# A hybrid attention trunk on one core: matmul order of all heads written out, and three smaller edits

## The chip, the cores and the metric

The kernel runs on one core of a Trainium2 chip. The core has a matmul engine (PE, TensorE), three engines for elementwise work (VectorE or DVE, ScalarE or ACT, GpSimd or POOL), a queue that issues transfers (SP) and 16 DMA engines. The engines run side by side, each through its own list of instructions in order, and wait for each other through semaphores. The metric is the device time of one execution in microseconds (us). The kernel before takes 1009.78 us, the median of three runs (1008.76 to 1011.21).

## What is computed

Four layers act on x, 512 tokens by 1024 features in float32. Layer 0 and 3 use latent attention (MLA), layer 1 a sliding window of 128 with sinks (SWA), layer 2 forgetting attention (FoX). Each has 16 heads, a SiLU gate on the heads' outputs, an output projection, and a residual with a layer norm. Cut to what matters:

```python
def _mla_branch(x, w_in, q_norm, w_q_up, kv_norm, w_kv_up, w_out):
    h = x @ w_in                                   # cq 384, ckv 256, k_rope 32, gate 1024
    q = (_rmsnorm(cq, q_norm) @ w_q_up).reshape(B, S, 16, 64 + 32)
    kv = (_rmsnorm(ckv, kv_norm) @ w_kv_up).reshape(B, S, 16, 64 + 64)
    q_rope = _apply_rope(q[..., 64:], cos, sin)
    k_rope = _apply_rope(k_rope, cos, sin)         # one rotated key of 32, shared by all heads
    o = _dense_causal(q_full, k_full, v, 96 ** -0.5)
    return (o * silu(gate)) @ w_out

def _apply_rope(x, cos, sin):
    x1, x2 = split(x, 2)
    return concat([x1 * cos - x2 * sin, x2 * cos + x1 * sin])
# SWA: 16 query heads on 4 key heads, 128-query blocks against 256 keys, ALiBi; the sink joins the maximum:
    m = maximum(max(s), sink); p = exp(s - m) / (sum(exp(s - m)) + exp(sink - m))
# FoX: dense causal softmax with a cumulative log forget gate added to the scores
# every layer: x = layernorm(alpha * x + branch(x))
```

## The kernel before, in words

**Tiles.** Every float32 operand of a matmul is split into a rounded part and a remainder (fp32r), and a product is made of three matmuls (two for scores whose halves are stacked). Weights come from memory in units of up to 128 x 1024 by SP; ACT makes the rounded part (L291) and GpSimd, or VectorE for the output projection, the remainder (L295). `W` asks for a unit and has the following three prepared too (L302). A projection writes one bank of PSUM (three banks rotate, tag pp) and is then taken out by ACT and VectorE.

**A head.** Four score blocks s0 to s3 (one for each 128 queries, L450 or L903); after each a masked minimum on VectorE (L843, L904, L1023 and L1025; the scores are negated, so it stands for the maximum). `softmax_tail` (L415) is emitted after s3: in SWA the sink minimum (L419), exponentials on ACT with sums (L421), in SWA the sink's term (L424, L425), the reciprocal (L427), and the scaling of the first three blocks on GpSimd (L432) and of the last on ACT (L430). Then the probabilities are transposed on the matmul engine: three groups t0, t1, t2 (keys 0, 1, and 2 with 3) in MLA and FoX, two groups in SWA. t0 needs all four blocks in MLA and FoX, the first three in SWA. Each group is taken from its bank by ACT (L466) and VectorE (L467, remainder at L310). The product with V (pv, `attn_pv`) uses one bank; its result is added up by ACT and VectorE (L504, L505), and after each second head multiplied with the gate on GpSimd (L512) and split into oT for the output projection.

**Order.** `run_heads` (L614) emits, for h from 0 to 13, the scores of head h + 1, then the transposes and pv of head h, and between them steps of one stream: the projections of the later heads in the order of STREAM, then the first part of the output projection (`out_part`). FILLS holds how many steps go into each head. This emission order sets priorities; a planner that replays the program with its own costs settles the order on every engine, matmul too, and ANCHOR holds each stream step behind a named step of an earlier head (`held`). Only the last two heads (`tail`) and the start of MLA have the matmul order as written. FINISH is a written order for the end of a layer; its f entries run further steps of the output projection.

**MLA's start.** `t_block` makes cq, ckv and the shared key for each block of 128 tokens in two units of 352 columns: 672 columns of weights and, a second time, the 32 key columns with their halves swapped. `t_norm` scales, and rotates the key by four VectorE operations on 64 or 32 columns (L740 to L744), which also write its negative. `tr_kr` transposes the result (L774). V is projected in four units of 256 columns, each for four heads (`vproj`, `vp`).

Of the kernel before, what the change touches and what calls it, by code (L numbers as in the profile page):

```python
# [46 lines left out]
ANCHOR = (('s', 0), ('s0', 0), ('s', 1), ('o', 2))  # L47
TAIL = ((3, 4, 6, 6), (2, 10, 2, 5), (9, 0, 4, 9), (6, 3, 7, 2))
# [3 lines left out]
T_COLS = 352  # L52
# [3 lines left out]
def jobs(s):  # L56
# [11 lines left out]
FILLS = (  # L68
# [4 lines left out]
)  # L73


def layer_units(kind):
# [8 lines left out]
    for n, a in FIRST[kind] + STREAM[kind]:  # L85
        if kind == 0 and n in "KQR":
            p = 2 * a if n == "R" else a
            new = [("QK", p, 0, 640 if p % 2 else SUB)]
        elif kind == 0 and n == "V":
            new = [("V", a, 0, 512)]  # L90
        else:
            new = [("V", a, b, SUB) for b in range(2)] if n == "V" else [(n, a, 0, SUB)]
# [16 lines left out]
def pack_weights(inp):  # L109
# [8 lines left out]
    for (layer, n, a, b), off, c in units:  # L118
        kind, j = layer % 3, layer // 3
        if kind == 0:  # L120
            w_in, w_out = inp["mla_w_in"][j], inp["mla_w_out"][j]
            if n == "T":
                ro = QR + KR
                kr = w_in[:, ro:ro + 32]
                ks = np.concatenate([kr[:, 16:], kr[:, :16]], 1)
                w = np.concatenate([w_in[:, :ro], kr, ks], 1)[:, a * T_COLS:(a + 1) * T_COLS]
# [11 lines left out]
            elif n == "V":  # L138
                wv = inp["mla_w_kv_up"][j].reshape(KR, H, 128)[:, 4 * a:4 * a + 4, 64:].reshape(KR, 256)
# [25 lines left out]
def shape_consts():  # L165
# [7 lines left out]
    cc = np.concatenate([cos, cos, cos, -cos], 1)  # L173
    ss = np.concatenate([sin, sin, -sin, sin], 1)
    krt = np.stack([cc, ss], 1).reshape(NT, 128, 2, 64).transpose(1, 0, 2, 3).astype(np.float32)
# [12 lines left out]
class Net:  # L188
    def __init__(self, ctx, tc, t):
# [32 lines left out]
        self.cq_free = 0  # L222
        self.hold = len(units)
# [82 lines left out]
    def mm(self, out, l, r, start, stop):  # L306
        self.last = self.nc.tensor.matmul(out, l, r, start=start, stop=stop).ins  # L307
# [87 lines left out]
    def vproj(self, keys, nk, lhs, store, qd, tbs=range(NT), extra=None):  # L395
        per = -(-nk // len(keys))
        n = VF_COLS if extra else 256
        ps = None
        for tb in tbs:
            ws = [self.W(*k) for k in keys]  # L400
            if qd not in store:
                store[qd] = self.p_vo.tile([128, NT, 4, 128], F32R, tag="vo", name=self.nm("v"))
            if tb % 2 == 0 or extra or ps is None:
                ps = self.bank()
            c0 = 0 if extra else tb % 2 * 256
            out = ps[:, c0:c0 + n]
            yield from self.tokproj_steps(out, lambda k: (ws[k // per], (k % per) * n), n, lhs, tb, range(nk), True, True,
                                            8 if nk == 8 else 6)
            self.v_fin(store[qd], out[:, :256], tb)
# [203 lines left out]

    def run_heads(self, layer, st, make, pre=iter(()), npre=3):  # L614

        st["order"] = chain(chain.from_iterable(make[n](a) for n, a in STREAM[layer % 3]), self.out_part(layer, st))
        st["P"], st["PT"], st["oT"] = {}, {}, []
        marks = {}
        what, lag = ANCHOR[layer]

        def held(gen, h):

            after = marks.get((what, h - lag))
            with self.tc.issue_after(after) if after is not None else nullcontext():
                next(gen, None)

# [3 lines left out]
        marks["s", 0] = self.last  # L630
        self.run(pre)
        for h in range(H - 2):
            sn, tn = st["s_fn"](h + 1, st), st["t_fn"](h, st)
# [463 lines left out]
```

## Time and profile before

| | |
|---|---|
| median of three runs | 1009.78 us |
| the profiled execution's own time | 1010.33 us |
| its span, first to last instruction | 1008.5 us |
| mean granted matmul clock | 0.992 |
| PE busy | 981.8 us, 97%, 5512 matmuls |
| weight loads (PEld) busy | 857.3 us, 85% |
| DVE, ACT, POOL busy | 607.1, 620.8, 501.3 us |
| DMA | 117.31 MB |

The busy times are of one profiled execution. Busy time of PE is the union of matmuls that overlap in the pipeline; the time between starts of neighbouring matmuls tells how fast they go. A row of a group names line, engine, operation, tile written <- tiles read, shape and count, then busy us and mean ns of one, then the engine's idle time before them. In the timeline a row holds start, length, engine, line, operation, tiles, shape and count of neighbouring instructions put together. MLA's first pairs and heads lie at about 61 to 220 us, SWA's at 294 to 424, FoX's at 524 to 722, the second MLA's at 808 to 957.

### The profile page before, as it was taken

The numbers are of one execution on the slowest core, as the hardware profiler recorded it, in microseconds if no ns is written. First come the engines' busy times: TensorE is split into PE (matmuls) and PEld (weight loads), VectorE is DVE, ScalarE is ACT, GpSimd is POOL, SyncE is SP. The second block draws the span as 40 slices with busy tenths as digits, with TensorE's granted clock in tenths as the row PEclk, the third lists the DMA queues.
The fourth block names the chain that finished last, engine by engine and source line by source line (L and its number), as shares of the span: only waits on it lengthen the run. The fifth ranks groups of instructions, "written<-read, shape, count | busy, mean of one in ns | idle before, by whom it ended". The sixth has DMA issues, their size and how long they took to land.

```text
span 1008.5 us, 16186 instructions
## 1 busy us (share of the span) xinstructions
PE 981.8 (97%) x5512; PEld 857.3 (85%) x5512; DVE 607.1 (60%) x1533; ACT 620.8 (62%) x1354; POOL 501.3 (50%) x524
## 2 busy tenths in 40 slices
PE   8999999999999999999999999999999999999995
PEld 7988898888988888788988898888789888888784
DVE  2567666854636667729324655567457676668727
ACT  4378798854256777723446766566433588888722
POOL 4645665334145663423455757553252656664213
PEclk9999999999999999999999999999999999999998
DMA  6353333552542222334344334325234444324312
GB/s 222 125 140 105 92 103 95 150 172 97 188 126 84 80 68 102 111 92 158 96 141 131 105 85 145 106 78 192 88 104 136 121 130 125 97 84 134 97 64 84
DMA packets 37795, 117.31 MB, mean 116 GB/s; under 512 B 5440, under 2 KB 5440, under 8 KB 37456
## 3 DMA queue, kind: packets, MB, share of 16 engines
q1 hardware_dynamic: 37712, 116.27, 37.7%
q8 instruction: 44, 0.72, 0.3%
q14 instruction: 39, 0.32, 0.1%
HBM read 93.15 MB, written 8.42 MB: 101 GB/s over the span
## 4 chain that ended last, share of the span: by engine, by line
PE 48%; DVE 2%; issue 2%; ACT 1%; POOL 1%; DMA 0%; SPq 0%; DVEq 0%; POOLq 0%; ACTq 0%
PE pp L307 32%; PE ss L307 5%; PE oo L307 4%; PE po L307 4%; PE ptt L480 3%; DVE r L594 1%; POOL r L610 1%; PE pxt L357 1%; DMA q<-rq 0%; DVE r L546 0%; PE pc L764 0%; DVE w L295 0%; ACT wo L291 0%; DVE kt L310 0%; DVE wo L295 0%
## 5 line engine op out<-in xcount | busy, mean ns | idle before, releaser
L307 PE MATMUL pp<-xT,w 128*128 128x512 f32 (+1 forms) x1440 | 352.6, 387 | 0.1
L295 POOL TENSOR_TENSOR w<-wr,w 128x512 fp32r<-128x512 f32 (+1 forms) x202 | 242.5, 1226 | 197.0 <-ACT w L291 125.7
L307 PEld LDWEIGHTS pp<-xT,w 128*128 128x128 f32 x1440 | 256.2, 188 | 44.5 <-ACT xT L361 0.3
L432 POOL TENSOR_TENSOR P<-P,rs 128x256 f32<-128x256 f32 (+2 forms) x192 | 112.9, 616 | 134.5 <-DVE rs L427 130.8
L291 ACT CAST w<-wr 128x1024 fp32r<-128x1024 f32 (+5 forms) x121 | 116.6, 967 | 84.4 <-PE pp L307 44.1
L421 ACT ACTIVATE P<-P,m 128x256 f32<-128x256 f32 (+3 forms) x256 | 137.8, 539 | 47.6 <-DVE m L843 16.8
L310 DVE TENSOR_TENSOR PT<-ptt,PT 128x384 fp32r<-128x384 f32 (+1 forms) x176 | 103.7, 600 | 46.5 <-ACT PT L466 45.2
L307 PE MATMUL pp<-w,xT 128*128 128x256 f32 (+2 forms) x768 | 114.3, 302 | 3.1 <-ACT xT L361 2.5
L307 PEld LDWEIGHTS pp<-w,xT 128*128 128x128 f32 x768 | 107.4, 190 | 4.9 <-ACT xT L361 2.9
L466 ACT CAST PT<-ptt 128x384 fp32r<-128x384 f32 (+1 forms) x176 | 88.2, 515 | 35.3 <-PE ptt L480 24.8
L307 PE MATMUL oo<-PT,v 128*128 128x256 f32 (+3 forms) x512 | 106.6, 313 | 3.1 <-DVE o L505 2.9
L307 PEld LDWEIGHTS oo<-PT,v 128*128 128x128 f32 x512 | 83.4, 189 | 13.8 <-DVE o L505 3.4
L307 PE MATMUL ss<-kt,q 128*128 128x128 f32 (+3 forms) x384 | 81.5, 328 | 2.3 <-ACT kt L796 1.6
L307 PE MATMUL pp<-cT,w 128*128 128x512 f32 x312 | 81.6, 397 | 0.0
L480 PE MATMUL ptt<-ident,P 128*128 128x128 f32 x480 | 79.3, 277 | 1.3 <-POOL P L432 1.3
L307 PE MATMUL pp<-w,oT 128*128 128x512 f32 x288 | 76.4, 400 | 0.0
L843 DVE CUSTOM_DVE_ANT_0 P<-ss,mask 128x128 f32<-128x128 f32 (+3 forms) x128 | 60.9, 484 | 25.2 <-PE ss L307 20.7
L307 PE MATMUL po<-wo,oT 128*128 128x512 f32 x288 | 71.5, 396 | 0.0
L307 PEld LDWEIGHTS ss<-kt,q 128*128 128x128 f32 x384 | 60.6, 189 | 8.7 <-ACT kt L796 2.2
L480 PEld LDWEIGHTS ptt<-ident,P 128*128 128x128 f32 x480 | 57.7, 142 | 11.1 <-POOL P L432 1.8
L505 DVE TENSOR_TENSOR o<-oo,o 64x512 f32<-64x512 f32 x64 | 43.9, 686 | 38.0 <-ACT o L504 34.0
L307 PEld LDWEIGHTS pp<-cT,w 128*128 128x128 f32 x312 | 56.6, 188 | 10.3
(121 smaller groups left out, 1427.5 us busy)
## 6 DMA issues: line engine op xcount, KB each, us to landing
wr<-in_w SPq DMA_DIRECT2D x106, 512.0 KB, 3.6
q<-rq SPq DMA_DIRECT2D x64, 128.0 KB, 2.4
xd<-r SPq DMA_DIRECT2D x12, 512.0 KB, 2.8
r<-xd SPq DMA_DIRECT2D x12, 512.0 KB, 3.5
wr<-in_w SPq DMA_DIRECT2D x16, 352.0 KB, 3.5
kd<-kd SPq DMA_DIRECT2D x20, 256.0 KB, 3.0
tq<-in_cs SPq DMA_DIRECT2D x8, 512.0 KB, 3.8
cb<-cd SPq DMA_DIRECT2D x16, 256.0 KB, 3.7
```

Of the source, the lines that this page charges most:

```text
L291: nc.scalar.copy(w[0][:, :c], r[:, :c])
L295: eng.tensor_tensor(w[1][:, a:b], r[:, a:b], w[0][:, a:b].bitcast(F32), op=ALU.subtract)
L307: self.last = self.nc.tensor.matmul(out, l, r, start=start, stop=stop).ins
L310: (eng or self.nc.vector).tensor_tensor(out, src, hi.bitcast(F32), op=ALU.subtract)
L357: nc.tensor.transpose(v, xt[:, c:c + 128], self.ident[:])
L421: nc.scalar.activation(v, v, AF.Exp, bias=m[:, c:c + 1], scale=-1.0, accum_out=sums[:, c:c + 1])
L432: nc.gpsimd.tensor_tensor(v, v, rs[:, c:c + 1].to_broadcast([128, v.shape[1]]), op=ALU.mult)
L466: nc.scalar.copy(pt[:, 0, :n], ps[:, :n])
L480: nc.tensor.transpose(ps[:, c:c + 128], Ps[qb][:, kb * 128:(kb + 1) * 128], self.ident[:])
L505: nc.vector.tensor_tensor(o[a, :], o_ps[a, :], o[a, :], op=ALU.add)
L594: nc.vector.scalar_tensor_tensor(r[:, cols], in0=src[:, cols], scalar=s[:, k:k + 1], in1=st["gb"][2 * part + c][:], op0=op, op1=(ALU.mult, ...
L843: nc.vector.tensor_tensor_reduce(out=P[:, :n], in0=ps[:, :n], in1=self.mask[:, S - n:], scale=1.0, scalar=3e38, op0=ALU.add, op1=ALU.min, ...
```

## The change

- **Order of the heads.** `run_heads` puts all heads under a written matmul order. STREAM, FILLS, ANCHOR and `tail` give way to PAIRS: for each pair of heads, the projections that are made during it. The steps of a head stand as s0 s1 t0 s2 t1 s3 t2 pv (s of head h + 1, the others of head h; without t2 in SWA), and after each step so much of the pair's projections is emitted that their columns keep up with the share of steps done. EXTRA steps of the output projection join in the last pair; TAIL tells the steps of it after each step of the last two heads. The other engines are still ordered by the planner.
- **336-column units.** The swapped copy of the key columns is no longer projected; T_COLS is 336.
- **Key rotation on GpSimd.** Two products of 32 columns and four sums or differences of 16 in place of four VectorE operations.
- **512-wide V in MLA.** Two units of 512 columns, each for eight heads; the first is made ahead of the pairs and the second in the second pair.
- FINISH of layer 3 starts with f22 in place of f14.

```diff
-    'f14 k0 k1 k2 f99 r0 r1 s0 s1 ...
+    'f22 k0 k1 k2 f99 r0 r1 s0 s1 ...
...
-ANCHOR = (('s', 0), ('s0', 0), ('s', 1), ('o', 2))
-TAIL = ((3, 4, 6, 6), (2, 10, 2, 5), (9, 0, 4, 9), (6, 3, 7, 2))
+
+TAIL = (
+    (1, 1, 1, 1, 1, 1, 2, 3, 2, 2, 3),
+    (1, 1, 2, 1, 2, 2, 3, 3, 3),
+    (2, 1, 2, 1, 2, 1, 2, 3, 3, 2, 3),
+    (1, 1, 1, 1, 1, 1, 2, 3, 2, 2, 3),
+)
...
-T_COLS = 352
+T_COLS = 336
...
-STREAM = (
-    jobs("K1 Q1 R1 K2 Q2 V1 G2 K3 Q3 G3 R2 K4 Q4 V2 G4 K5 Q5 G5 R3 K6 Q6 V3 G6 K7 Q7 G7"),
-    jobs("G0 Q2 G1 Q3 G2 Q4 G3 Q5 G4 Q6 G5 Q7 G6 G7"),
-    jobs("Q2 K2 Q3 K3 G2 Q4 K4 V2 G3 Q5 K5 G4 Q6 K6 G5 V3 Q7 K7 G6 G7"),
+PAIRS = (
+    ("K1 Q1 R1 G2", "K2 Q2 V1", "K3 Q3 R2 G3", "K4 Q4 G4", "K5 Q5 R3 G5", "K6 Q6 G6", "K7 Q7 G7"),
+    ("G0 Q2", "G1 Q3", "G2 Q4", "G3 Q5", "G4 Q6", "G5 Q7", "G6 G7"),
+    ("V2 Q2 K2", "G2 Q3 K3", "G3 Q4 K4", "V3 Q5 K5", "G4 Q6 K6", "G5 Q7 K7", "G6 G7"),
 )
+STREAM = tuple(jobs(" ".join(k)) for k in PAIRS)
+
+EXTRA = (3, 0, 8, 3)
...
     def mm(self, out, l, r, start, stop):
-        self.last = self.nc.tensor.matmul(out, l, r, start=start, stop=stop).ins
+        self.nc.tensor.matmul(out, l, r, start=start, stop=stop)
+        self.cols += max(256, out.shape[-1])
...
+    def job_cols(self, kind, n, a):
+
+        if kind == 0 and n in "KQR":
+            return (6 if n == "K" else 9) * 512
+        return 96 * 256 if n == "V" and kind else 24 * 512
+
+    def slots(self, layer, st, h):
+
+        sn = st["s_fn"](h + 1, st) if h + 1 < H else []
+        tn = st["t_fn"](h, st)
+        out = sn[:2] + tn[:1] + sn[2:3] + tn[1:2] + sn[3:] + tn[2:]
+        return out + [lambda: self.attn_pv(h, st)]
+
     def run_heads(self, layer, st, make, pre=iter(()), npre=3):
 
-        st["order"] = chain(chain.from_iterable(make[n](a) for n, a in STREAM[layer % 3]), self.out_part(layer, st))
+        with self.tc.manual_schedule(engines={mybir.EngineType.PE}):
+            self.heads(layer, st, make, pre, npre)
+
+    def heads(self, layer, st, make, pre, npre):
+        kind = layer % 3
+        st["order"] = self.out_part(layer, st)
...
+        for p in range(NP - 1):
+            todo = jobs(PAIRS[kind][p])
+            total = sum(self.job_cols(kind, n, a) for n, a in todo)
+            gen = chain.from_iterable(make[n](a) for n, a in todo)
+            if p == NP - 2:
+                gen = chain(gen, islice(st["order"], EXTRA[layer]))
+                total += EXTRA[layer] * 3 * 512
+            done = i = 0
+            for h in (2 * p, 2 * p + 1):
+                steps = self.slots(layer, st, h)
+                for f in steps:
                     f()
+                    i += 1
+                    while done + 768 < total * i / (2 * len(steps)):
+                        c = self.cols
+                        if next(gen, self) is self:
+                            break
+                        done += self.cols - c
+            self.run(gen)
+        self.cq_done(layer)
+        steps = self.slots(layer, st, H - 2) + self.slots(layer, st, H - 1)
+        for f, n in zip_longest(steps, TAIL[layer], fillvalue=0):
+            f()
+            self.run(islice(st["order"], n))
         self.finish(layer, st)
...
-            a, b = x[:, 640:704], x[:, 704:768]
-            nc.vector.tensor_tensor(b, a, krt[:, tb, 1, :], op=ALU.mult)
-            nc.vector.tensor_tensor(a, a, krt[:, tb, 0, :], op=ALU.mult)
-            nc.vector.tensor_tensor(x[:, 768:800], x[:, 640:672], x[:, 736:768], op=ALU.add)
-            nc.vector.tensor_tensor(x[:, 800:832], x[:, 672:704], x[:, 704:736], op=ALU.add)
+            kr, c, d = x[:, 640:672], x[:, 672:704], x[:, 704:736]
+            nc.gpsimd.tensor_tensor(c, kr, krt[:, tb, 0, :], op=ALU.mult)
+            nc.gpsimd.tensor_tensor(d, kr, krt[:, tb, 1, :], op=ALU.mult)
+            c1, c2, d1, d2 = x[:, 672:688], x[:, 688:704], x[:, 704:720], x[:, 720:736]
+            for o, l, r, op in ((768, c1, d2, ALU.subtract), (784, c2, d1, ALU.add), (800, c2, d1, ALU.add), (816, d2, c1, ALU.subtract)):
+                nc.gpsimd.tensor_tensor(x[:, o:o + 16], l, r, op=op)
...
-        vp = lambda qd, tbs=range(NT): self.vproj([(layer, "V", qd, 0)], 2, vlhs, vs, qd, tbs)
+        vp = lambda a, tbs=range(NT): self.vproj([(layer, "V", a, 0)], 2, vlhs, vs, (2 * a, 2 * a + 1), tbs)
```

`vproj` now takes a list of groups of four heads: for MLA it makes 512 columns per block in a bank of its own, and hands each half to its group's `v_fin` (ACT and VectorE).

More of the change, by code (lines that the diff above doesn't have):

```diff
@@ L1 @@
 import math
-from contextlib import ExitStack, nullcontext
-from itertools import chain, islice
+from contextlib import ExitStack
+from itertools import chain, islice, zip_longest
 import numpy as np
@@ L89, in layer_units @@
         elif kind == 0 and n == "V":
-            new = [("V", a, 0, 512)]
+            new = [("V", a, 0, SUB)]
         else:
@@ L222, in __init__ @@
         self.cq_free = 0
+        self.cols = 0
         self.hold = len(units)
@@ L984, in fox @@
         vs, qt, kt = {}, {}, {}
-        vp = lambda qd, tbs=range(NT): self.vproj([(layer, "V", qd, 0), (layer, "V", qd, 1)], 8, self.xblk, vs, qd, tbs)
+        vp = lambda a, tbs=range(NT): self.vproj([(layer, "V", a, b) for b in range(2)], 8, self.xblk, vs, (a,), tbs)
         z = self.p_g.tile([128, NT, H], F32, tag="g", name=self.nm("z"))
@@ L992, in fox @@
         for tb in range(NT):
-            self.run(self.vproj([(layer, "V", 0, b) for b in range(3)], 8, self.xblk, vs, 0, [tb], f_logit))
+            self.run(self.vproj([(layer, "V", 0, b) for b in range(3)], 8, self.xblk, vs, (0,), [tb], f_logit))
             self.run(vp(1, [tb]))
```

72 lines of the change are left out of this document (18 added, 54 removed), and 6 rows, old and new, of tables (FILLS, FINISH).

## The prediction

> **What bounds the kernel now.** I read the page first, then the waits of the matmul engine, then the merged chain that ended last. The page's busy line, and its shares of the chain by engine and by line:
>
> ```profile
> PE 981.8 (97%) x5512; PEld 857.3 (85%) x5512; DVE 607.1 (60%) x1533; ACT 620.8 (62%) x1354; POOL 501.3 (50%) x524
> ...
> PE 48%; DVE 2%; issue 2%; ACT 1%; POOL 1%; DMA 0%; SPq 0%; DVEq 0%; POOLq 0%; ACTq 0%
> ```
>
> Matmul is on the chain far more than any other engine. The waits of that engine over the whole span (total us, times, longest):
>
> ```profile
> PE oo L307 <- DVE o L505: 2.9, 2, 1.6
> PE pp L307 <- ACT xT L361: 2.5, 1, 2.5
> PE pxt L357 <- DVE r L594: 2.4, 4, 1.0
> PE ss L307 <- DVE m L904: 1.6, 3, 0.7
> PE ss L307 <- ACT kt L796: 1.6, 2, 0.8
> ...
> PE ptt L480 <- POOL P L432: 1.3, 3, 0.6
> PE ss L307 <- DVE m L843: 0.8, 3, 0.4
> ```
>
> They are small: what a new order of the heads can win back is oo 2.9 + ss 1.6 + ptt 1.3 + ss 0.8 = 6.6 us; xT, pxt and kt belong to the stages between and to the first scores of a layer. That the engine is full when it does not wait shows in the merged chain (start, length, count):
>
> ```profile
> 538.58 0.76 PE ptt L480 x7
> ...
> 584.26 2.93 PE pp L307 x24
> ...
> 734.87 8.30 PE po L307 x36
> ```
>
> The first are transposes, at 0.76/7 = 0.109 us each, the second 256-column matmuls at 2.93/24 = 0.122 us, the third 512-column ones at 8.30/36 = 0.231 us. I use these spacings below, since the busy times of single matmuls overlap. The heads are therefore bound by matmul issue, and any wait that a rigid order adds there is added to the end.
>
> **Columns saved.** Groups by form:
>
> ```profile
> L307 PE MATMUL pp<-xT,w 128*128 128x512 f32 x1344 | 339.7, 394 | 0.0
> L307 PE MATMUL pp<-w,xT 128*128 128x352 f32 x288 | 50.6, 329 | 3.1 <-ACT xT L361 2.5 <-DVE xT L310 0.3 <-ACT w L291 0.3
> L307 PE MATMUL pp<-w,cT 128*128 128x256 f32 x192 | 28.7, 286 | 0.1
> ```
>
> From 352 to 512 columns a matmul gets (394 - 329)/160 = 0.41 ns per column longer, so 16 columns less are 6.5 ns. There are 2 layers x 4 blocks x 2 units x 24 = 384 of them: **-2.5 us**. V of MLA goes from 192 matmuls of 256 to 96 of 512: 192 x 0.122 - 96 x 0.231 = **-1.2 us**. Part of V moves out of the pairs' stream into the stage ahead of the heads; that is a shift on the same engine and costs nothing more. The weight casts and subtractions become fewer or shorter.
>
> The Trainium skill ("Trainium Kernel Development and Optimization", Performance Expectations, and "Perfetto Trace Analysis", Identifying the Most-Contended Engine) says that matmul busy time is a bad measure and that the busy share of weight loads is a good one. By that rule the 85% above would leave some 15% of the span free, both this saving and the waits below could vanish in it, and the sum would be zero; by the spacing of the chain the engine is full and they count in whole.
>
> **Rotation of the shared key.** Four VectorE operations per block become six on GpSimd, of 32 and 16 columns. The nearest rows:
>
> ```profile
> L743 DVE TENSOR_TENSOR cqk<-cqk 128x32 f32<-128x32 f32 x8 | 3.4, 427 | 0.0
> ...
> L295 POOL TENSOR_TENSOR w<-wr,w 128x32 fp32r<-128x32 f32 x1 | 0.3, 257 | 0.0
> ```
>
> Six at up to 0.26 us are 1.5 us a block on GpSimd. Its reader is the transpose pkr, late in this piece of the matmul timeline:
>
> ```profile
> 44.95 5.63 PE L307 MATMUL pp<-xT,w 128*128 128x512 f32 x24
> ...
> 61.31 0.60 PE L774 MATMUL pkr<-ident,cqk 128*64 128x128 f32 x4
> ```
>
> The last block is projected before 44.95 and read at 61.31: 16 us of gate, transposes and projections cover it. Queued behind it on GpSimd are weight remainders loaded three units ahead. I take zero; with the cover gone it would be 1.5 us in each of two layers, 3 us.
>
> **The order of the heads.** Now the three transposes, the four score blocks and the product with V of neighbouring heads stand in a fixed row: s0 s1 t0 s2 t1 s3 t2 pv, s of head h+1, t and pv of head h, with projections cut into equal shares after each (SWA has no t2). Matmul cannot pass a step whose operand is late; the whole rest of the row queues behind it. Two distances decide.
>
> *First, s3 to the next t0 (softmax).* In SWA a pair has 12 pieces of 4 matmuls (0.92 us) for 14 steps; counting the loop out, one piece follows each step but t1. From the start of the last matmul of s3 to t0: its own slot 0.12, piece 0.92, pv 6 x 0.122 + 2 x 0.109 = 0.95, piece 0.92, s0 0.22, piece 0.92, s1 0.24, piece 0.92 = **5.2 us** (128-column scores taken at the transposes' spacing). What softmax needs is seen where it met least competition, head 0 of SWA, timeline:
>
> ```profile
> 296.74 0.63 PE L307 MATMUL ss<-kd,q 128*128 128x256 f32 x4
> 297.52 0.42 DVE L904 CUSTOM_DVE_ANT_0 P<-ss,ali 128x256 f32<-128x256 f32 x1
> ...
> 297.98 0.23 DVE L419 TENSOR_SCALAR m<-m,nsink 128x4 f32<-128x4 f32 x1
> ...
> 298.25 0.40 ACT L421 ACTIVATE P<-P,m 128x128 f32<-128x128 f32 x1 [2.23 <-DVE m L419]
> ...
> 300.12 0.28 ACT L424 ACTIVATE es<-m,sink 128x4 f32<-128x4 f32 x1
> ...
> 300.63 0.18 DVE L427 RECIPROCAL rs<-sm 128x4 f32<-128x4 f32 x1
> 300.96 1.54 POOL L432 TENSOR_TENSOR P<-P,rs 128x128 f32<-128x128 f32 x3 [4.56 <-DVE rs L427]
> ```
>
> The last of the four scores starts about 0.28 before 297.37, at 297.09; the scaled probabilities are there at 302.50: **5.4 us**, and the transpose may follow some 0.1 later. So even the free chain is 0.3 late. All four exponentials wait for the sink minimum (L419), so none starts early. In a busier head:
>
> ```profile
> 367.34 0.40 PE L307 MATMUL ss<-kd,q 128*128 128x256 f32 x2
> ...
> 368.72 1.26 DVE L419 TENSOR_SCALAR m<-m,nsink 128x4 f32<-128x4 f32 x1
> ...
> 372.72 1.54 POOL L432 TENSOR_TENSOR P<-P,rs 128x128 f32<-128x128 f32 x3 [2.77 <-DVE rs L427]
> ```
>
> There it is 374.26 - 367.45 = 6.8 us. In the new row t1 stands straight before s3, and its remainder on VectorE (0.55 us, row below) comes just ahead of L419: I take 5.4 + 0.5, that is 5.9 + 0.1 against 5.2, a wait of 0.8 us. For 13 heads 10.4, and 1.3 + 1.5 for the last two, whose fill is thinner: **+13.2 us**. Bounds: 0.3 a head and thinner at the end, 5.7 us; 1.7 a head, 26.7 us. What is late next: pv, s0 and s1 of the following head shift with it, so the loop does not catch up.
>
> In MLA and FoX the exponentials of the first three blocks run before s3. MLA, timeline:
>
> ```profile
> 138.29 0.85 PE L307 MATMUL ss<-kt,q 128*128 128x512 f32 x3
> ...
> 139.50 0.48 ACT L466 CAST PT<-ptt 128x384 fp32r<-128x384 f32 x1 [0.36 <-PE ptt L480]
> ...
> 139.87 0.69 DVE L843 CUSTOM_DVE_ANT_0 P<-ss,mask 128x512 f32<-128x512 f32 x1
> ...
> 140.49 0.55 DVE L310 TENSOR_TENSOR PT<-ptt,PT 128x384 fp32r<-128x384 f32 x1
> 140.61 0.72 ACT L421 ACTIVATE P<-P,m 128x512 f32<-128x512 f32 x1
> ...
> 141.77 1.76 POOL L432 TENSOR_TENSOR P<-P,rs 128x128 f32<-128x128 f32 x3 [2.74 <-DVE rs L427]
> ```
>
> From the minimum at 139.87 to 143.53 are 3.7 us, with 0.45 before it 4.1. The same count of slots gives 5.0 to 6.4 us in MLA (pieces of 0.69 or 0.92) and 6.8 to 8.8 in FoX. No wait is taken; with 1.4 more, as SWA's two heads differ, 5.5 would exceed the short MLA gaps a little, about 2 us a layer.
>
> *Second, t2 to the end of pv.* The last bank goes through ACT (0.48) and VectorE (0.55) before pv can use it. In MLA the exponential of s3 stands ahead of that copy: from the last score matmul 0.45 + 0.69 + 0.05, then exponential to 1.9, copy to 2.4, remainder to about 3.1. Counting slots, pv wants the remainder after 2.2 to 3.5, 2.85 in most heads; over 15 heads the lack is 4.4 us, both MLA layers **+8.8 us**. Below it nothing, if the copy is put first; above it, a weight cast in between in half the heads, 7 us a layer more, 22.8 in all. That ACT is loaded there shows in the stage rows (PE, PEld, DVE, ACT, POOL):
>
> ```profile
> 61.00:220.00 159.00, 157.60 (x908) 137.40 (x907) 114.70 (x283) 133.12 (x298) 89.26 (x98) 1.00 0.45 128
> ...
> 294.00:424.00 130.00, 126.56 (x717) 109.71 (x715) 88.50 (x248) 93.74 (x239) 68.68 (x80) 0.99 0.26 84
> ```
>
> 133.12/159 is 84% in MLA. FoX has pieces of 0.9 us or more between these steps: zero, up to 3 us.
>
> *Waits that go.* Evenly spread scores and pvs end most bunching: of the 6.6 us I count oo 2.9 and ss 1.6, **-4.5 us**; between 0 and 6.6.
>
> **Sum.** The profiled execution took 1010.3 us (span 1008.5, 1.8 around it). 1010.3 - 2.5 - 1.2 - 4.5 + 13.2 + 8.8 = 1024.1. It stood 0.5 above the median of 1009.8, so the forecast is **1023.5 us**.
>
> **Rivals.** *Faster:* the planner still orders VectorE, ACT and GpSimd and may serve softmax so early that the SWA wait stays at or below 0.3 and MLA has none: 1009.8 - 8.2 + 0 to 5.7 = 1002 to 1007, about 1004. Break-even is at 8.2/15 = 0.55 us a head, a chain of 5.65 us instead of 5.9, which is near; against it, the free chain is already longer than the gap. *Crowded:* each SWA head runs like the 6.8 us one and MLA's copies meet weight casts: 1009.8 - 8.2 + 26.7 + 17 (three quarters of the 22.8) = 1045. For it ACT's 84%; against it, every wait of matmul gives the others time. *No change:* savings and waits cancel, or matmul has room that the waits fill: 1009.8. The second way is what the rule on weight loads says; the spacing of 0.231 us in the chain speaks against it, so of the 0.12 below it has 0.03. That the columns are not saved at all would add 3.7 us to any of these.
>
> **Chances.** Forecast 0.40, faster 0.36, crowded 0.12, no change 0.12. A measurement of this kernel can tell about 0.2%, 2 us. So faster 0.36, same 0.12, slower 0.52. The forecast's own range is 1013 to 1035; with the others, 1000 to 1042, leaving 0.08 below and 0.10 above.
>
> **What would show it.** Right: matmul's waits in SWA name its transposes waiting for the scaling on GpSimd, 6 to 25 us in all; in MLA pv waits for PT of L310; 5416 matmuls, 384 of them with 336 columns; pkr waits for nothing. Wrong: the SWA window stays at 130 us with such waits under 3 us, or softmax chains well under 5.2 us from s3; then the order costs nothing and the saving stands alone.

## The result and the profile after

The changed kernel takes 1094.9 us (median of four runs, 1092.7 to 1096.6), the kernel before 1009.3 beside it: a ratio of **1.0844** (95%: 1.0815 to 1.0872). It is slower, as forecast, but by 86 us where 14 were forecast, and outside the range. The profile's span and its busy line after:

```profile
span 1094.8 us, 15923 instructions
...
PE 1021.4 (93%) x5416; PEld 855.1 (78%) x5416; DVE 603.9 (55%) x1501; ACT 626.3 (57%) x1350; POOL 509.0 (46%) x572
```

There are 96 matmuls fewer, and the weight loads, ACT and VectorE are about as busy as before; only the time is longer. The waits of the matmul engine (total us, times, longest):

```profile
PE oo L305 <- DVE PT L309: 16.1, 39, 2.3
PE ptt L931 <- POOL P L435: 14.5, 25, 1.9
PE ptt L483 <- POOL P L435: 5.5, 13, 1.0
PE oo L305 <- ACT PT L469: 4.7, 10, 0.8
PE pxt L356 <- DVE r L597: 4.6, 5, 2.2
PE pp L305 <- DVE v L391: 4.4, 3, 3.2
PE ss L305 <- DVE m L910: 3.5, 6, 0.9
```

The two waits that the prediction named lead the list: pv for PT of the remainder helper (now L309), and SWA's transposes (L931) for the scaling on GpSimd (now L435). But all rows of this view, these seven and six smaller ones, make some 60 us, since the modelled end of the matmul before covers part of each gap. A fuller account takes, from the timeline, the distance of each matmul's start to the next, less the usual distance for its columns (0.228 us for 512, 0.118 for 256, 0.109 for a transpose), and puts it down to what released the late one; I call the sum **excess**. It is 34.4 us before and 124.4 after, so 90.0 more. The spans differ by 1094.8 - 1008.5 = 86.3; the other 3.7 are about what the smaller edits save in matmul work. That the two agree follows from how the sum is made: it tells where the time lies, and not yet why. By stages (length from the first score matmul to the last pv matmul, us):

| stage | length before | after | excess before | after | largest parts after |
|---|---|---|---|---|---|
| MLA 0 | 165.9 | 177.1 | 3.9 | 20.9 | oo for PT 11.1 |
| SWA | 147.2 | 173.3 | 7.1 | 42.4 | ptt for P 23.8, oo for PT 6.3, ss for m 4.4 |
| FoX | 210.0 | 222.4 | 5.0 | 22.8 | ptt for P 5.5, pp for v 5.1, oo for PT 4.9 |
| MLA 3 | 165.2 | 176.6 | 4.8 | 22.4 | oo for PT 11.2 |
| all between | 320.2 | 345.4 | 13.6 | 15.9 | |

The last row grows by 25 us, 2 of them excess: output projection steps were moved there out of the heads. The heads have that much less to do and are 61 us longer.

**SWA.** One head takes 10.5 us (transposes start at 380.14 and 390.66) where it took about 8.7 before (309.59 to 405.00 for eleven heads). Timeline of one period, scores to the next transpose:

```profile
383.73 1.05 ACT L289 CAST w<-wr 128x1024 fp32r<-128x1024 f32 x1 [0.61 <-PE pp L305]
...
383.78 0.48 PE L305 MATMUL ss<-kd,q 128*128 128x256 f32 x2
...
384.77 0.23 DVE L422 TENSOR_SCALAR m<-m,nsink 128x4 f32<-128x4 f32 x1
...
385.06 0.40 ACT L424 ACTIVATE P<-P,m 128x128 f32<-128x128 f32 x1
...
387.45 0.18 DVE L430 RECIPROCAL rs<-sm 128x4 f32<-128x4 f32 x1
...
387.71 2.53 POOL L293 TENSOR_TENSOR w<-wr,w 128x512 fp32r<-128x512 f32 x2 [3.22 <-ACT es L427]
...
390.21 0.96 POOL L435 TENSOR_TENSOR P<-P,rs 128x128 f32<-128x128 f32 x2
...
390.66 0.33 PE L931 MATMUL ptt<-ident,P 128*128 128x128 f32 x1 [0.77 <-POOL P L435]
```

The reciprocal is there at 387.63, 3.7 us after the last score, and the scaling could begin. Ahead of it in GpSimd's list stand two weight remainders, 2.53 us together. So the chain, up to the end of the scaling's third block (391.74, past this view), is 7.8 us long, not the 5.9 of the forecast. (The transposes start after the first scaled block, at 390.66, and wait for the others one by one; the forecast let them wait for all three.) In the instruction list the remainder of a unit waits for the last matmul of the unit four before, whose tiles it takes. Here that matmul is done at 387.59, just as the scaling falls due, and the planner put the remainder first. With the even spread it comes at this step in every head.

**MLA.** The same timeline in one head:

```profile
178.74 0.69 DVE L849 CUSTOM_DVE_ANT_0 P<-ss,mask 128x512 f32<-128x512 f32 x1 [0.54 <-PE ss L305]
...
179.23 0.49 PE L483 MATMUL ptt<-ident,P 128*128 128x128 f32 x3
179.27 1.05 ACT L289 CAST w<-wr 128x1024 fp32r<-128x1024 f32 x1
...
180.34 0.59 ACT L830 ACTIVATE q<-pp 64x512 fp32r<-64x512 f32 x1
...
180.84 0.71 ACT L424 ACTIVATE P<-P,m 128x512 f32<-128x512 f32 x1
...
181.54 0.46 ACT L469 CAST PT<-ptt 128x384 fp32r<-128x384 f32 x1
...
182.06 0.39 PE L305 MATMUL oo<-PT,v 128*128 128x256 f32 x1 [0.59 <-ACT PT L469]
...
183.23 0.56 PE L305 MATMUL oo<-PT,v 128*128 128x256 f32 x3 [0.79 <-DVE PT L309]
```

The exponential is due at 179.4 and the copy of PT at 179.7; a cast and a copy of q are ahead of both on ACT, and pv waits twice.

**FoX.** V has two 256-column blocks in a bank, and the second must wait until the first is taken out:

```profile
666.22 1.27 POOL L515 TENSOR_TENSOR o<-o,g 128x512 f32<-128x512 f32 x1
...
667.52 0.62 ACT L516 CAST oT<-o 128x512 fp32r<-128x512 f32 x1 [0.80 <-POOL o L515]
668.05 0.38 ACT L390 ACTIVATE v<-pp 128x256 fp32r<-128x256 f32 x1
...
668.46 0.42 DVE L391 SCALAR_TENSOR_TENSOR v<-pp,v 128x256 fp32r<-128x256 f32 x1 [1.01 <-ACT v L390]
668.94 2.45 PE L305 MATMUL pp<-w,xT 128*128 128x256 f32 x11 [3.16 <-DVE v L391]
```

ACT holds V's copy behind a cast that waits for GpSimd; the matmul row stands still for over 3 us.

### The profile page after: what moved, and what is told of

It is laid out like the page before. It is cut to its first block, busy times and chain, and to the rows that moved or that the text cites. A ratio compares the mean times of both kernels' runs of the same rounds, so it can differ in the third digit from the quotient of the medians.

```text
span 1094.8 us, 15923 instructions
## 1 busy us (share of the span) xinstructions
PE 1021.4 (93%) x5416; PEld 855.1 (78%) x5416; DVE 603.9 (55%) x1501; ACT 626.3 (57%) x1350; POOL 509.0 (46%) x572
## 5 line engine op out<-in xcount | busy, mean ns | idle before, releaser
L305 PE MATMUL pp<-xT,w 128*128 128x512 f32 (+1 forms) x1440 | 378.1, 395 | 0.1
L293 POOL TENSOR_TENSOR w<-wr,w 128x512 fp32r<-128x512 f32 x202 | 241.5, 1221 | 224.3 <-ACT w L289 126.4
L305 PEld LDWEIGHTS pp<-xT,w 128*128 128x128 f32 x1440 | 251.4, 191 | 37.7 <-ACT xT L360 0.3
L435 POOL TENSOR_TENSOR P<-P,rs 128x256 f32<-128x256 f32 (+2 forms) x192 | 114.2, 623 | 189.4 <-DVE rs L430 168.0
L289 ACT CAST w<-wr 128x1024 fp32r<-128x1024 f32 (+4 forms) x117 | 115.4, 990 | 101.6 <-PE pp L305 39.1
L309 DVE TENSOR_TENSOR PT<-ptt,PT 128x384 fp32r<-128x384 f32 (+1 forms) x176 | 106.1, 603 | 103.8 <-ACT PT L469 103.1
L305 PE MATMUL oo<-PT,v 128*128 128x256 f32 (+3 forms) x512 | 101.3, 321 | 20.9 <-DVE PT L309 16.1
L305 PEld LDWEIGHTS oo<-PT,v 128*128 128x128 f32 x512 | 83.2, 189 | 45.3 <-DVE PT L309 26.7
L305 PE MATMUL pp<-cT,w 128*128 128x512 f32 x312 | 91.0, 405 | 0.0
L483 PEld LDWEIGHTS ptt<-ident,P 128*128 128x128 f32 x480 | 61.4, 141 | 27.8 <-POOL P L435 10.4
L305 PE MATMUL pp<-w,oT 128*128 128x512 f32 x288 | 82.3, 414 | 0.0
L305 PEld LDWEIGHTS ss<-kt,q 128*128 128x128 f32 x384 | 66.5, 194 | 15.3 <-ACT kt L802 3.6
L305 PEld LDWEIGHTS po<-wo,oT 128*128 128x128 f32 x288 | 53.6, 188 | 11.8
```

Source lines behind the costliest of these rows:

```text
L289: nc.scalar.copy(w[0][:, :c], r[:, :c])
L293: eng.tensor_tensor(w[1][:, a:b], r[:, a:b], w[0][:, a:b].bitcast(F32), op=ALU.subtract)
L309: (eng or self.nc.vector).tensor_tensor(out, src, hi.bitcast(F32), op=ALU.subtract)
L435: nc.gpsimd.tensor_tensor(v, v, rs[:, c:c + 1].to_broadcast([128, v.shape[1]]), op=ALU.mult)
L483: nc.tensor.transpose(ps[:, c:c + 128], Ps[qb][:, kb * 128:(kb + 1) * 128], self.ident[:])
```

## The experiments

Three theories. **D**: distances in the fixed row are too short. **Q**: the order on ACT and GpSimd is at fault, weights ahead of the urgent step. **S**: the even spread is. Times are of one run unless an interval is given; the kernel before took 1008.8 to 1010.3 beside them.

**e1_cols.** The kernel before with the two small edits alone.

```diff
-T_COLS = 352
+T_COLS = 336
...
-            nc.vector.tensor_tensor(b, a, krt[:, tb, 1, :], op=ALU.mult)
...
+            nc.gpsimd.tensor_tensor(c, kr, krt[:, tb, 0, :], op=ALU.mult)
+            nc.gpsimd.tensor_tensor(d, kr, krt[:, tb, 1, :], op=ALU.mult)
...
```

> The kernel before with only the 336-column units and the key rotation on GpSimd; order of the heads as before. Both theories on the heads agree here: 384 matmuls shorter by 6.5 ns each are 2.5 us, the rotation is covered, so 1006.8 us, within 1005.5 to 1008. If the planner is upset by the small edit, it can move by several us either way, and the order of the heads is then sensitive in itself.

1008.8 us, ratio 0.9986 (0.9975 to 0.9998): 1.4 us gained by the ratio, less than expected. The stretch up to the first scores is 2.2 us shorter; 2.1 are lost ahead of the second MLA, where x's transposes wait 1.7 us for r. These two edits don't cost; the wide V and FINISH were not run alone. No other version here takes as little time as the kernel before.

**e2_free.** The changed kernel, TensorE's order left to the planner up to the last two heads.

```diff
-        with self.tc.manual_schedule(engines={mybir.EngineType.PE}):
-            self.heads(layer, st, make, pre, npre)
+        self.heads(layer, st, make, pre, npre)
+        with self.tc.manual_schedule(engines={mybir.EngineType.PE}):
+            self.tail(layer, st)
```

> The changed kernel, with the same emission order in the pairs, but matmul ordered by the planner there (the last two heads stay written). Theory D (distance: the written row leaves softmax and the copies of the transposed probabilities too little matmul work to hide behind, and a matmul engine that cannot pass the late step loses the time): most of the 85 us comes back, 1010 to 1030. Theory Q (queues: ACT and GpSimd are given weight preparation ahead of the urgent step because of where the units end; matmul order is secondary): most stays, 1060 to 1095. Theory S (even spreading is the harm, fixed or not): stays at 1095.

1039.3 us. SWA falls from 173.3 to 153.3, FoX from 222.4 to 204.1, each MLA by 10. Of the 86 us 56 hang on TensorE keeping to the written row. 30 stay with all else that changed in the heads: the even spread, the new order of the projections, the missing ANCHOR holds, and some 24 us of output projection that now run behind the heads. These were not taken apart; "spread" below stands for all of them.

**e3_look2.** Weights prepared two units ahead instead of three.

```diff
-        self._split(max(i, min(i + 3, self.hold)))
+        self._split(max(i, min(i + self.ahead, self.hold)))
...
+        self.ahead = 2
```

> The changed kernel with weights split two units ahead instead of three while the pairs run: a unit's remainder then no longer becomes possible at the very moment in which the unit before the current one ends. In SWA the two remainder subtractions of 1.27 us stood ahead of the scaling and the scaling ended 7.8 us after s3. Theory Q: in SWA the scaling starts right after the reciprocal, 5.3 us after s3, the period of a head falls from 10.5 to 8.2 to 8.7 us, 25 to 35 us come back there, 1060 to 1070 in all. Theory D: the chain stays over 5.2 us by itself, at most 10 us come back, 1085 to 1095.

1093.7 us, nothing moved; the remainders stand ahead of the scaling as before. The tiles, not the look-ahead, tell when a remainder can start, so this was no test of Q.

**e4_sfirst.** All scores ahead of the transposes.

```diff
-        out = sn[:2] + tn[:1] + sn[2:3] + tn[1:2] + sn[3:] + tn[2:]
+        out = sn + tn
```

> The changed kernel with all four score steps ahead of the transposes in the written row (s0 s1 s2 s3 t0 t1 t2 pv), still fixed and evenly spread. From s3 to the next t0 there are then about 8 us in SWA and 8 to 9 in MLA instead of 5.2 and 5.0 to 6.4; from the last transposes to pv the same one share as in the changed kernel. Theory D: waits of the transposes for the scaling vanish (20 us in the waits view), those of pv for the copies stay or grow: 1050 to 1070. Theory Q: GpSimd's scaling moves later with the order, the waits stay: 1080 to 1095.

1124.7 us, worse than either expectation. In SWA the transposes' wait for the scaling fell from 23.8 to 0.5 of excess, as D has it, but others came. Its waits of the matmul engine:

```profile
PE oo L305 <- ACT PT L469: 21.1, 33, 2.0
PE ptt L483 <- DVE PT L309: 19.1, 21, 1.8
PE oo L305 <- DVE PT L309: 15.5, 44, 1.4
```

Here PT's copy is late: ACT's exponentials run from 383.38 to 385.26 in one period, and the copy follows at 385.44. A longer distance in one place was paid for in another.

**e5_gap.** An empty step, so one more share, between t2 and pv.

```diff
-        return out + [lambda: self.attn_pv(h, st)]
+        return out + [lambda: None, lambda: self.attn_pv(h, st)]
```

> The changed kernel, with one more step in each head's row, an empty one between the last transposes (t2) and pv: the projections' shares fall to a ninth of a pair's half each instead of an eighth, and one of them stands between t2 and pv. Theory D (the distances of the fixed row are too short): the copies of PT have one share more time (some 0.7 to 1 us), so pv's waits for PT go, of which by the spacing of matmuls 11 us lie in each MLA layer, 8 in SWA and 5 in FoX; softmax's wait in SWA stays, as s3 to t0 is not made longer by more than the cut of the shares takes back. Sum 20 to 30 us: 1065 to 1075. Theory Q (order on ACT and GpSimd, weights ahead of the urgent step): the casts move with the row, the copies stay behind them, and at most 10 us are won: 1083 to 1095.

1076.7 us: 18 gained, a little short of D's figure. MLA gains 5 a layer (oo for PT 11.1 to 6.6), FoX 10; in SWA oo's wait goes (6.3 to 1.0) but ptt's grows (23.8 to 27.3), length 172.9.

**e6_behind.** GpSimd's remainders are issued behind the scaling emitted last.

```diff
+            behind = getattr(self, "scaled", None) if eng is nc.gpsimd else None
+            with self.tc.issue_after(behind) if behind is not None else ExitStack():
+                for a in range(0, c, 512):
...
-                nc.gpsimd.tensor_tensor(v, v, rs[:, c:c + 1].to_broadcast([128, v.shape[1]]), op=ALU.mult)
+                self.scaled = nc.gpsimd.tensor_tensor(v, v, rs[:, c:c + 1].to_broadcast([128, v.shape[1]]), op=ALU.mult).ins
```

> The changed kernel, with GpSimd's weight remainders ordered behind the last softmax scaling written so far (order of issue alone, no wait, no other work). In SWA two remainders of 2.5 us together stand ahead of the scaling of every head in the changed kernel. Theory Q: the first transposes get their scaled blocks 2.5 us earlier, the SWA period falls from 10.5 to about 8.8 us, ptt's waits for GpSimd (about 24 us of spacing in SWA, 5.5 in FoX, 3.6 in MLA) fall to a quarter: 1066 to 1075. Theory D: the 5.3 us that the softmax chain takes without the remainders are still more than the row gives (about 4.9 us), half of the waits stay, the stall turns up in the next wait of the row: 1080 to 1092. If the remainders then come late for their own matmuls, pp waits for them and nothing is won: 1090 to 1100.

1080.2 us: 15 gained, at the lower end of D's range. All of it is SWA (173.3 to 156.5; ptt for P 23.8 to 9.1), so the remainders were the larger part of that wait; MLA and FoX stay within 3 us, against what Q expected there.

**e7_both.** ACT's weight casts behind ACT's last scaling of the softmax as well.

```diff
+            soft = getattr(self, "soft", None)
+            with self.tc.issue_after(soft) if soft is not None else ExitStack():
+                nc.scalar.copy(w[0][:, :c], r[:, :c])
...
+                self.soft = nc.scalar.activation(v, v, AF.Copy, scale=rs[:, c:c + 1]).ins
```

> As the run before it, and ScalarE's weight casts ordered behind the last ScalarE scaling of the softmax written so far as well. Theory Q: in MLA the exponentials and the copy of PT no longer stand behind a cast of 1.05 us, so that pv's waits there fall from 11 to about 5 us a layer: 8 to 12 us less than with the remainders alone, 1055 to 1065. Theory D: the cast then meets the copies of PT of the following transposes, the waits only change places: within 5 us of the run with the remainders alone.

1049.1 us: 31 us less than with the remainders alone, more than any theory gave. Each MLA drops (176.6 to 166.5, 174.5 to 168.8; oo for PT from 11.2 to 4.0 in the first), SWA to 151.9, FoX by 10.

**e10_casts.** The casts alone, GpSimd left free; against e7:

```diff
-            behind = getattr(self, "scaled", None) if eng is nc.gpsimd else None
+            behind = None
```

> The changed kernel, with ScalarE's weight casts alone ordered behind the last ScalarE scaling of the softmax; GpSimd's order is left free. A remainder reads its cast, so it can't come ahead of the softmax either. Theory Q with the cast as the lever: 1045 to 1055, as the run with both orders (1049). If the two orders do separate things, 1060 to 1070: both together (46 us) less the 15 of the remainders alone.

1050.3 us, as with both: **the cast is the lever**, since a remainder follows its cast. SWA's timeline now:

```profile
363.17 0.50 PE L309 MATMUL ss<-kd,q 128*128 128x256 f32 x2
...
367.72 0.18 DVE L434 RECIPROCAL rs<-sm 128x4 f32<-128x4 f32 x1
...
368.04 1.54 POOL L439 TENSOR_TENSOR P<-P,rs 128x128 f32<-128x128 f32 x3 [2.78 <-DVE rs L434]
```

0.14 us lie between reciprocal and scaling, where 2.58 did.

**e9_both_gap.** Both orders and the empty step: the lines of e5, e6 and e7.

> Both orders (remainders behind the scaling, casts behind ScalarE's part of the softmax) and the empty step between t2 and pv. If waits for scaling and waits for PT are two separate things, the gains add: 1065 to 1075 for the gap alone and 20 to 30 for the orders give 1035 to 1050, and what is left against 1009 is the spread itself (the kernel with the order left free stood at 1039). If both are one slack that a fixed row lacks, the gains overlap: 1055 to 1070.

1035.6 us, in the range for gains that add; they overlap in part (45.9 for the orders, 18.2 for the step, 59.3 together). MLA is at 164.4 and 166.6 us, SWA at 144.9, FoX at 213.9.

**e11_free_both.** Order left free, with both orders of the weights: the lines of e2, e6 and e7.

> TensorE's order left free in the pairs (1039 us with the orders of weights free) and both orders of the weights behind the softmax. If the 30 us that were left there are the same cause (weights ahead of the softmax, which an even spread makes due at the same step of each head), they go: 1010 to 1020, no wait of more than 5 us in a stage beside those of the kernel before. If they come of the spread itself (units that end together, no slack where the softmax needs it), 1030 to 1040.

1033.5 us: 6 gained, not 20 to 30. With TensorE's order free the casts are the smaller part of what costs; the 25 us left come with the spread, in SWA (excess 18.4, 7.1 before) and both MLA layers (10.8 and 12.0, 3.9 and 4.8 before).

**e12_own.** e9 with a bank for each block of V.

```diff
-            if tb % 2 == 0 or n > 256 or ps is None:
-                ps = self.bank()
-            c0 = 0 if n > 256 else tb % 2 * 256
+            ps = self.bank()
+            c0 = 0
```

> The best of the kernels with the fixed row so far (both orders, empty step; 1035.6 us), and V's two blocks of 256 columns in FoX each in a bank of its own. The matmuls of the second block then don't wait until VectorE has emptied the first (pp waits for v: 4.5 us of spacing in FoX): 1030 to 1033 if the bank was the cause. If the wait only moves to the next one for the bank that is now used twice as often, 1035 to 1037.

1029.5 us: 6 gained, pp's wait for v is gone; FoX is 3.4 us shorter. The rest is in the second MLA (166.6 to 163.8).

**e13_gap2.** e9 with two empty steps.

```diff
-        return out + [lambda: None, lambda: self.attn_pv(h, st)]
+        return out + [lambda: None] * 2 + [lambda: self.attn_pv(h, st)]
```

> The same best kernel with two empty steps between t2 and pv. Theory D: both distances grow (s3 to t0 from six ninths to seven tenths of a head, t2 to pv by a further share of 0.7 to 0.9 us), and the waits of ptt (14 us) and of oo for PT (6 us) fall by half: 1024 to 1030. If the waits that are left come from the order on the other engines and not from the distance: 1033 to 1038.

1040.1 us, against D. MLA gains (161.8, 161.2) but SWA goes from 144.9 to 151.9: ss now waits 5.1 us for m and ptt 7.9 for P. No one distance suits all stages.

**f1_fixrow.** The kernel before with its TensorE order written as the changed kernel's row, uneven counts kept.

```diff
-            slots = [(sn[:2], "s0"), (sn[2:3], ""), (sn[3:], "s")] + [([t], "") for t in tn] + [([], "")]
-            slots += [([lambda: self.attn_pv(h, st)], "o")]
...
+        with self.tc.manual_schedule(engines={mybir.EngineType.PE}):
+                steps = sn[:2] + tn[:1] + sn[2:3] + tn[1:2] + sn[3:] + tn[2:] + [lambda: self.attn_pv(h, st)]
+                for i, f in enumerate(steps):
+                    f()
+                    n = (total * (i + 1) + len(steps) - 1) // len(steps) - done
+                    self.run(islice(st["order"], n))
```

> The kernel before, with TensorE's order in the heads written as the changed kernel's row (s0 s1 t0 s2 t1 s3 t2 pv), but its own uneven counts of projection steps behind each step of a head; nothing else of the change. With the order left free the uneven kernel takes 1009 and the evenly spread one 1039; with the order fixed the spread one takes 1095. If fixing the order costs by itself what it cost there (55 us): 1055 to 1075. If the even spread and the fixed row cost only together (weights fall due in each head just at the softmax): 1015 to 1030.

1105.5 us, above both expectations. Projections run further ahead of s3 here, so that scores of some heads probably take the keys of a later pair, and what this kernel computes is not the reference's function. Only its time is used, and f5 repeats the question without this.

**f2_fixrow_casts.** The same, with e7's lines for the casts; what is said of f1's scores holds here too.

> As the run before it (fixed row, uneven counts), with ScalarE's weight casts ordered behind the last ScalarE scaling of the softmax. If casts ahead of the softmax are what a fixed row can't stand, whatever the spread: 20 to 35 us less than without, as in the changed kernel (45 of 85). If the uneven counts already put the casts elsewhere: within 5 us of it.

1094.9 us: 11 gained, between the two expectations. With uneven counts casts are the smaller part; pp's wait for v is the largest in MLA (11.1 and 12.0 of excess).

**f5_fixrow2.** f1 in a wider row, with the projections where they stood to scores and pv before.

```diff
+                steps = [sn[:2], tn[:1] + sn[2:3], tn[1:2] + sn[3:], [], [], tn[2:], [], [lambda: self.attn_pv(h, st)]]
```

> The kernel before with TensorE's order fixed and its uneven counts, in a wider row: s0 s1, a share, t0 s2, a share, t1 s3, three shares, t2, two shares, pv, a share. The projections stand to scores and pv as in the kernel before (in the first fixed row with uneven counts they ran ahead of s3, so that scores of some MLA heads could take the keys of a later pair, and that kernel's computation is not quite the reference's). From s3 to the next t0 lie seven eighths of a head's projections, from t2 to pv two. If a fixed order costs because distances are short, this row takes most of the 96 us back: 1015 to 1040. If a fixed order costs by itself, since the other engines' order was planned for another one: 1055 to 1090.

1094.9 us. **A written row costs 86 us without the even spread too**, just above the range given for that. It is not shown that any fixed order costs so much: a row copied from the planner's own order was not tried. ptt's wait in SWA is down to 4.3, but ss waits 15.4 for m there and pp 8.3 and 9.9 for v in MLA.

**f6_bunched.** e12 in this wider row.

> The best kernel with the fixed row (casts and remainders behind the softmax, V's blocks in a bank each, even shares: 1029.5), its heads in the same wider row; its last two heads are left as they are. If distance is what it still lacks, ptt's waits (13 us over the stages) and oo's (6 us) go: 1008 to 1016. If the bunched scores then wait for their banks (ss for m), 1022 to 1032, as with two empty steps (1040 without V's banks).

1061.4 us, 32 worse, and worse than either expectation. Its waits:

```profile
PE ss L309 <- DVE m L915: 12.0, 18, 1.6
PE oo L309 <- DVE PT L313: 8.1, 21, 1.6
...
PE ptt L486 <- POOL P L438: 2.7, 7, 0.5
PE ptt L936 <- POOL P L438: 1.0, 1, 1.0
```

The softmax's wait went down, and in SWA, 8.5 us longer, the bunched scores wait for VectorE to empty their banks. The MLA layers lose 10 us each (164.3 to 174.3 and 163.8 to 173.6), of which pv's wait for PT and the scores' wait for q make most. D alone falls with this.

**f3_cols_casts.** e1 with e7's lines for the casts, order free.

> The kernel before with 336-column units and the rotation on GpSimd (1008.8), and the weight casts ordered behind the softmax, TensorE's order left free. There casts in front of the softmax are worked around by TensorE's own order and cost little: within 2 us of 1008.8. If they cost here too (excess of 7 us in SWA, 4 to 5 in each MLA layer), 1000 to 1006.

1014.6 us, ratio to before 1.0057 (1.0036 to 1.0077): 0.6% longer, about 6 us above e1. SWA gains 3 us, the first MLA loses 5 (a projection waits 2.9 us for oT on GpSimd). The order that gains 45 us in the fixed row costs a little in the free order of the kernel before; in the free order of e2 it gained 6 (e11).

**f4_mix.** Each stage by the best seen: two empty steps in MLA, one in SWA, FoX free, own banks, both orders; against e11, beside e12's lines:

```diff
+        with self.tc.manual_schedule(engines={mybir.EngineType.PE}) if layer % 3 != 2 else ExitStack():
...
+        return out + [lambda: None] * (2, 1, 0)[layer % 3] + [lambda: self.attn_pv(h, st)]
```

> The evenly spread kernel, each stage by the best that the runs showed: casts and remainders behind the softmax everywhere, two empty steps before pv in MLA (161.5 us a layer), one in SWA (144.9), in FoX the order free (201.8) and V's blocks in a bank each. If stages don't act on each other the lengths add: 1029.5 less 5 less 9 = 1014 to 1018. If a stage's backlog of weights is handed on to the next, 1020 to 1030.

1020.8 us, at the edge of the second expectation. Excess 48.5 against 34.4 before, of it 16.1 in SWA, where the kernel before has 7.1: that stage is the larger part of what stays. Why SWA reached 144.9 in e9 and e12 and 147.1 here was not tried.

The square, in us:

| | order free | order fixed |
|---|---|---|
| uneven counts | 1009 (before) | 1105 (f1), 1095 (f5) |
| even spread | 1039 (e2) | 1095 (changed kernel) |
| even spread, casts and remainders behind the softmax | 1034 (e11) | 1049 (e7); 1029 with the empty step and V's banks too (e12) |

## Why the prediction was wrong in size

**Columns, V, rotation: right as far as seen.** The usual distance of the start of a matmul to the next is 0.154 us for 336 columns where it was 0.161 for 352, which makes 2.7 us over 384 where 2.5 were forecast. In the groups by form the 336-column matmuls are 288 + 96 = 384, as forecast, and pkr starts with no wait. V's 1.2 us was not measured alone.

```profile
L305 PE MATMUL pp<-w,xT 128*128 128x336 f32 x288 | 50.1, 328 | 1.6 <-ACT xT L360 1.5
...
L305 PE MATMUL pp<-wo,xT 128*128 128x336 f32 x96 | 16.2, 317 | 0.0
```

```profile
59.65 0.60 PE L780 MATMUL pkr<-ident,cqk 128*64 128x128 f32 x4
```

**Waits that go: right in kind.** The wait of oo for o (2.9 us) is no longer on the list; the new ones outweigh it.

**First distance, +13.2 (up to 26.7): this step failed.** The place and the engine were right. The transposes' wait for the scaling, none in SWA before, is 23.8 us of excess after, inside the bound. The chain of 5.4 to 6.8 us was read in the planner's own order; in the fixed row it is 7.8, as the weight remainders (2.53) now fall due with the scaling. The forecast priced the distance of the row and not what would stand in GpSimd's list at that moment; e6 and e10 show that part. SWA's whole excess rose by 35.3: the forecast gave it no second distance, and pv waits 6.3 for PT and ss 4.4 for m.

**Second distance, +8.8 for both layers (up to 22.8): this step failed too.** pv's waits for PT are 11.1 and 11.2, just inside the bound. The case "a weight cast in between" was named, but kept for the bound; it is the rule (MLA fence above), and e7 and e10 take most of it back. The excess of the two layers rose by 17.0 and 17.6: the other 12 us had no term. They lie mostly in the transposes' waits for the scaling, 1.8 in each layer, and in stretches at half the granted clock (last section).

**FoX at zero (up to 3): wrong**, 17.8. Softmax's wait was argued from distance alone; V's shared bank was not looked at. e12 shows the bank, e2 (204.1) that a free order hides it all.

Together: of the 90 us of new excess the two waits that were priced make 46, twice their price of 22. The other 44 come from what was put at nothing.

**The rivals.** "Crowded" named the right mechanism with a chance of 0.12. Its 26.7 and 17 for the two waits come close to what they measured (23.8 and 22.3); at 1045 it was still 50 short because it too put the rest at nothing. "Faster" rested on the planner serving softmax early; it did the opposite. "No change" by slack in the engine fell: the weight loads took as long as before (855.1 us, 857.3 before) and the span grew by 86, so the 15% in which they were not busy was no room for waits. The Trainium skill ("Perfetto Trace Analysis", Identifying the Most-Contended Engine) takes the busy share of weight loads as a measure of how close a kernel is to the roofline. Here that share was 85% before the change, while the excess of matmul spacing was 34.4 of 1008.5 us: the share shows more room than the waits found.

**What is settled and what is not.** Settled: keeping TensorE to the written row is what costs (e2, f5), through waits on the other engines' lists. With the even spread the weight casts ahead of the softmax make 45 us of it (e10), and short distance with V's bank 20 more (e9, e12); with uneven counts the casts make 11 (f2). The spread, with what came with it, costs 25 to 30 us with a free order (e2, e11). Open: which part of the spread that is; what of the last 20 us in e12 is the row and what the spread; whether a row copied from the planner's own order, or other lists for the fixed row, would win them. Most of these figures come from one run each; four runs of the changed kernel lie 4 us apart, so differences of a few us are argued from the waits beside them.

## What to carry to other kernels

In a written order on the busiest engine, lateness on the others became lost time here, and the lists that the planner made for them put weights ahead of the urgent step. Write the lists that feed the row along with it, above all the weight preparation behind the softmax. Price such a change by what will stand ahead of the urgent instruction in its engine's list at that moment, not by chains read in the old schedule, and price every stage: half of the loss lay in what had no term. Moving one step of the row moves the wait (e4, e13, f6); look at all waits before and after, not at the one that was to go.

## What was not expected of the hardware

The granted matmul clock fell to half at seven places of the profile after, four before, behind gaps of the matmul engine; for 3.41 us at most of them, for 6.8 at one (1031.1). The last place lies at the end in each. Windows of core 0 (busy us of PE, PEld, DVE, ACT, POOL, then the clock, DMA share, GB/s):

```profile
450.00:454.00 4.00, 1.87 (x8) 1.05 (x7) 3.50 (x11) 2.31 (x5) 2.45 (x3) 1.00 0.44 135
454.00:457.50 3.50, 3.44 (x11) 2.62 (x12) 1.44 (x3) 1.46 (x2) 0.55 (x1) 0.53 0.52 163
...
665.00:669.00 4.00, 0.84 (x8) 0.61 (x7) 1.50 (x6) 2.09 (x5) 3.27 (x4) 1.00 0.82 220
669.00:672.50 3.50, 3.50 (x17) 3.50 (x18) 0.00 (x0) 0.00 (x0) 0.49 (x1) 0.54 0.05 16
```

After 1.87 us of work in 4.0, and after 0.84 in 4.0, the clock is 0.53 and 0.54. Such a place costs up to 1.7 us more than the wait itself. In the heads the clock was at half for 6.8 us before and 23.9 after, so this makes at most 8.5 us, an estimate, of what the heads lost. The Trainium skill ("TensorE: Matmul & The Clock Gate", Part 1: The HAM clock gate) has the clock halved after an idle window of about 3.4 us and back after a busy one of that length. The trace agrees on the half (0.53 and 0.54 over slightly longer windows) and on the length (3.41 us). What was not expected is that a window idle in part suffices: at 454 us the longest gap ahead is 1.70 us.

```profile
454.03 1.05 PE L931 MATMUL ptt<-ident,P 128*128 128x128 f32 x3 [1.70 <-POOL P L435]
```

No run was made to find the limit, but the traces bound it. All these changes fall on a grid of 3.41 us. In the traces of all kernels here, every grid window at full clock with less than 1.57 us of profiled matmul busy time was followed by the half clock, and none with more than 2.44 was; between them both occur.
